# High and low halves of the weights in one tile, column by column

## The chip, the cores and the metric

The kernel runs on one NeuronCore of one Trainium2 chip. The metric is the device time of one execution in microseconds (us). TensorE (PE) multiplies; a matmul there is two instructions, a weight load (PEld in the profile), which puts up to 128 columns of the stationary operand into the array, and the matmul proper, which streams the moving operand past them. ScalarE (ACT) and VectorE (DVE) do the elementwise work, SyncE (SP) issues the transfers, and SBUF is the memory on the chip from which PE reads both operands: 128 partitions, and in each of them a row of bytes.

## The reference

One inference step of one decoder layer over 304 rows (16 meta tokens, 256 prompt rows, 8 sequences of 4 sampled rows) and a model width of 2048. Cut to what matters here:

```python
z = rms_norm(x, norm_mix) @ w_in                 # 2048 -> 3360 (RWKV-7) + 4096 (retention)
o = concat(rwkv7_mixer(z[..., :3360]), retention_mixer(z[..., 3360:]))
h = x + o @ w_out                                # 2048 -> 2048
hn = rms_norm(h, norm_ffn)
h = h + (silu(hn @ w_gate) * (hn @ w_up)) @ w_down   # 2048 -> 5632 -> 2048
y = rms_norm(h, norm_final)
```

Everything is float32. The two mixers (a recurrence over 64-wide heads, and chunked retention) need small matmuls and much elementwise work; the five big products with `w_in`, `w_out`, `w_gate`, `w_up` and `w_down` are nearly all of the arithmetic.

## The kernel before

**Splitting in halves.** Each weight and each activation is split into a high half, rounded to float32r, and a low half, the rest that the rounding left. A product is the sum of three matmuls into one PSUM bank: high weights by high activations, high by low, low by high (`main`, lines 723 to 725). The stationary operand is a block of 128 by 128 weights, the moving one 288 to 304 columns of activations, one column for each row of the input.

**The stream of weights.** All weights lie in `big` in the order of their use, cut into pieces of 128 x 512. `load` brings a piece into a ring `wr` of WR = 5 raw tiles. `cast` (line 666) makes the two halves: ACT copies the piece into a tile `wh` of type float32r (the high half), and `rest` lets DVE write `wl` = raw - high (the low half). `wh` and `wl` are two rings of WS = 5 tiles of 512 columns, 2 KB a partition each. One piece feeds four blocks of 128 columns, so twelve matmuls. In `main`, ACT's cast of a piece is issued three pieces ahead of the one in use, and DVE's subtraction half a piece later; only for the first nine pieces, while the input itself arrives, is each piece cast just before use.

**What sets the order.** `steps` lists the matmuls of the five products in one fixed order. Around them a planner (`Plan`) runs a draft of the whole program against estimated costs, notes which of the mixers' streams to advance when, and the real program repeats these decisions; on each engine the order of the program is kept. The draft knows of each operand only the box from its first to its last element.

**Where the tiles lie.** Scratch tiles share two arenas, one for float32, one for float32r. `Room.place` packs them, the float32r arena first (at most `WIDE` words) and the float32 arena into the `ROOM` words less that. The float32 arena lies first and is padded with `GAP` words, so that the float32r arena behind it starts at a chosen place. It holds the feed-forward activations `act`, whose used part starts `SHIFT_A` words into the tile: 0, 4, 8, ... 32, then 2 and 6 for the eleven groups of four blocks of `w_down`. For the products with `w_gate` and `w_up` the moving operands `xh` and `xl` have `SHIFT_X` = 4 * (k // 2) words, k being the block of rows. A word is 4 bytes.

Of the kernel before, what the change touches and what calls it, by code (L numbers as in the profile page):

```python
# [8 lines left out]
F32 = mybir.dt.float32  # L9
F32R = mybir.dt.float32r  # L10
# [5 lines left out]
P = 128  # L16
# [31 lines left out]
WS = 5  # L48
# [31 lines left out]
LASTK = T - P  # L80
KEYS = ((0, META, SEQ, 0), (P, P, NP - P, SEQ), (LASTK, 2 * P, T - 2 * P, SEQ + NP - P))
RMW = SEQ + NP - P + T - 2 * P
ROOM = 33040
GAP = 56
WIDE = 4200
FREE, GAPS, TRIES = 800.0, (2000.0, 1000.0, 500.0, 200.0, 50.0, 0.0), 12

# [215 lines left out]
class Timed:  # L303


    def __init__(self, plan, eng, name):
        self._plan, self._eng, self._name = plan, eng, name
# [280 lines left out]
class Step:  # L588


    def __init__(self, tc, I, O, ctx, rooms, draft, log):
        self.tc, self.nc, self.I, self.O = tc, tc.nc, I, O
        self.rooms, self.draft = rooms, draft
        pool = lambda n, b, **k: ctx.enter_context(tc.tile_pool(name=n, bufs=b, **k))
        self.cp = pool("const", 1)
        self.wp = pool("weights", 1)
        self.mp = pool("scratch", 1)
        self.ap_ = pool("acc", ACC, space=bass.MemoryType.PSUM)
        self.pp = pool("psum", 8 - ACC, space=bass.MemoryType.PSUM)
        self.n, self.tags = 0, {}  # L600
        self.plan = pl = Plan(self.nc, rooms, draft, log, (lambda i: i) if draft else tc.keep_in_program_order)
        self.sp = pl.sp
        if not draft:
            self.arena = {dt: self.mp.tile([P, r.size + (GAP if dt == F32 else 0)], dt, tag=f"arena_{dt}", name=f"arena_{dt}")
                          for dt, r in rooms.items()}
        self.pe, self.dve, self.act, self.pool = pl.pe, pl.dve, pl.act, pl.pool
        pl.outside = {v.name for v in (*I.values(), *O.values())}
        self.outs = []
        self.live = 0
        self.done = set()  # L610
# [53 lines left out]
        self.loaded += n  # L664

    def cast(self, parts=1):
        hi = self.t([P, 512], "wh", F32R, pool=self.wp, bufs=WS)
        lo = self.t([P, 512], "wl", F32R, pool=self.wp, bufs=WS)
        o = self.halved % WCOLS
        raw = self.raws[0][:, o:o + 512]  # L670
        n = 512 // parts
        part = [slice(c * n, (c + 1) * n) for c in range(parts)]
        for c in part:
            self.act.copy(hi[:, c], raw[:, c])
        self.halves.append((hi, lo))
        self.rests.append((lo, [(lo[:, c], raw[:, c], hi[:, c]) for c in part]))
        self.halved += 512
        if o + 512 == WCOLS:
            self.raws.pop(0)
# [1168 lines left out]
def body(tc, I, O):  # L1848
# [6 lines left out]
    rooms[F32R].place(WIDE)  # L1855
    rooms[F32].place(ROOM - rooms[F32R].size)
    with ExitStack() as ctx:
# [23 lines left out]
```

## Time and profile before

| | |
|---|---|
| time, median of 3 runs (lowest to highest) | 1549.97 us (1548.45 to 1550.41) |
| the profiled execution's own time | 1547.98 us |
| its span in the profile | 1546.2 us |
| granted PE clock over the span | 0.997 |
| PE / PEld busy | 99% / 97% |
| DVE / ACT / POOL busy | 70% / 56% / 2% |

The page of the profile lists the busy time of each engine, the span in 40 slices, the chain of work that ended last, and groups of instructions by name and shape. A matmul's recorded duration is longer than its share of the array's time, since the next one starts before it ends; so the time that a matmul costs is read here from the distance of one start to the next, as the timeline gives it, or as length of a window over the number of matmuls in it.

The kernel has two parts. Until about 600 us the products with `w_in` and `w_out` run among the small matmuls of the mixers, and DVE is busy for most of the time; from there to 1506 us PE does the feed-forward products almost alone.

### The profile page before, as it was taken

What the parts mean: (1) busy time and instruction counts of PE and PEld (TensorE: products, weight loads), DVE (VectorE), ACT (ScalarE), POOL (GpSimd) and SP (SyncE); (2) the same over time, 40 slices, a digit from 0 to 9 for tenths busy, and PEclk for the clock granted to TensorE, in tenths of its full rate; (3) what the DMA queues carried; (4) which work ended last, traced back from release to release, by engine and by line L of the source; (5) the groups of instructions that cost most, each with busy time, mean ns of one, the idle gap of its engine ahead of it and who ended that gap; (6) DMA issues with size and microseconds to landing.
All of it is one profiled execution on the core that took longest, in us unless ns stands there. A gap on an engine that the chain in (4) does not pass through costs nothing.

```text
span 1546.2 us, 31919 instructions
## 1 busy us (share of the span) xinstructions
PE 1530.1 (99%) x11446; PEld 1502.8 (97%) x11446; DVE 1089.9 (70%) x2782; ACT 866.5 (56%) x2031; POOL 27.7 (2%) x161
## 2 busy tenths in 40 slices
PE   9999999999999999999999999999999999999997
PEld 8999999999999989999999999999999999999997
DVE  6998789898899878676555565656565656565656
ACT  6775876787877765554444444444444444444446
POOL 1000000000000000000000000000000000000000
PEclk9999999999999999999999999999999999999998
DMA  7554445445434575655555555555655555655553
GB/s 243 163 148 140 131 110 155 120 115 170 155 117 150 170 262 190 207 165 164 169 165 169 165 167 171 163 170 159 171 165 169 165 166 166 173 159 172 161 171 116
DMA packets 136334, 252.33 MB, mean 163 GB/s; under 512 B 15984, under 2 KB 22256, under 8 KB 136176
## 3 DMA queue, kind: packets, MB, share of 16 engines
q1 hardware_dynamic: 136176, 250.29, 54.6%
q8 instruction: 91, 1.49, 0.4%
q14 instruction: 67, 0.55, 0.1%
HBM read 235.95 MB, written 14.28 MB: 162 GB/s over the span
## 4 chain that ended last, share of the span: by engine, by line
PE 93%; DVE 5%; ACT 1%; issue 1%; DMA 0%; SPq 0%; DVEq 0%; ACTq 0%
PE acc L314 82%; PE mm L314 11%; DVE arena_dt.float L314 3%; DVE wl L314 1%; DMA arena_dt.float<-xT 0%; SPq L314 0%; ACT arena_dt.float L314 0%; DVE arena_dt.float32r L314 0%; ACT arena_dt.float32r L314 0%; ACT wh L314 0%; DVE xl L314 0%; ACT xh L314 0%; DVEq L1877 0%; ACT shout L314 0%; DVEq L314 0%
## 5 line engine op out<-in xcount | busy, mean ns | idle before, releaser
L314 PE MATMUL acc<-xh,wh 128*128 128x288 f32 (+2 forms) x2592 | 790.6, 305 | 1.8 <-ACT wh L314 1.0
L314 PE MATMUL acc<-xl,wh 128*128 128x288 f32 (+2 forms) x2592 | 768.5, 296 | 0.1
L314 PE MATMUL acc<-xh,wl 128*128 128x288 f32 (+2 forms) x2592 | 766.4, 296 | 0.3 <-DVE wl L314 0.3
L314 ACT CAST wh<-wr 128x512 fp32r<-128x512 f32 (+1 forms) x827 | 501.4, 616 | 352.7 <-PE acc L314 313.2
L314 DVE TENSOR_TENSOR wl<-wr,wh 128x512 fp32r<-128x512 f32 (+1 forms) x827 | 560.3, 685 | 130.6 <-ACT wh L314 127.8
L314 PEld LDWEIGHTS acc<-xh,wh 128*128 128x128 f32 x2592 | 487.2, 188 | 8.7 <-issue 3.7
L314 PEld LDWEIGHTS acc<-xl,wh 128*128 128x128 f32 x2592 | 486.3, 188 | 4.5 <-issue 1.2
L314 PEld LDWEIGHTS acc<-xh,wl 128*128 128x128 f32 x2592 | 485.8, 187 | 0.9 <-DVE wl L314 0.6
L314 PE MATMUL acc<-arena_dt.float32r,wh 128*128 128x288 f32 x1408 | 280.6, 295 | 0.4 <-ACT arena_dt.float32r L314 0.3
L314 PEld LDWEIGHTS acc<-arena_dt.float32r,wh 128*128 128x128 f32 x1408 | 225.9, 188 | 0.8 <-ACT arena_dt.float32r L314 0.5
L314 PE MATMUL acc<-arena_dt.float32r,wl 128*128 128x288 f32 x704 | 207.7, 295 | 0.0
L314 DVE TENSOR_TENSOR arena_dt.float<-acc,arena_dt.float 128x288 f32<-128x288 f32 (+4 forms) x181 | 72.7, 419 | 168.5 <-PE acc L314 168.2
L314 DVE TENSOR_TENSOR arena_dt.float<-arena_dt.float 128x288 f32<-128x288 f32 (+22 forms) x694 | 175.1, 286 | 12.0 <-ACT arena_dt.float L314 7.6
L314 ACT ACTIVATE arena_dt.float<-arena_dt.float 128x288 f32<-128x288 f32 (+7 forms) x245 | 104.6, 433 | 117.0 <-DVE arena_dt.float L314 115.2
L314 PE MATMUL mm<-arena_dt.float 128*128 128x128 f32 (+7 forms) x1136 | 167.7, 302 | 0.6 <-issue 0.2
L314 DVE TENSOR_TENSOR arena_dt.float<-arena_dt.float,acc 128x288 f32<-128x288 f32 (+1 forms) x210 | 94.6, 451 | 97.3 <-PE acc L314 97.0
L314 PEld LDWEIGHTS mm<-arena_dt.float 128*128 128x128 f32 (+1 forms) x1136 | 141.3, 181 | 11.3 <-issue 3.6
L314 PEld LDWEIGHTS acc<-arena_dt.float32r,wl 128*128 128x128 f32 x704 | 132.4, 188 | 0.0
L314 ACT COPY arena_dt.float<-mm 64x64 f32<-64x64 f32 (+11 forms) x330 | 91.5, 286 | 49.1 <-PE mm L314 44.0
L314 ACT CAST arena_dt.float32r<-arena_dt.float 128x288 fp32r<-128x288 f32 (+4 forms) x73 | 30.5, 423 | 90.8 <-DVE arena_dt.float L314 90.3
L314 ACT COPY arena_dt.float<-arena_dt.float 128x32 f32<-128x32 f32 (+7 forms) x235 | 57.1, 293 | 13.3 <-DVE arena_dt.float L314 11.5
L314 DVE SCALAR_TENSOR_TENSOR arena_dt.float<-arena_dt.float 128x288 f32<-128x288 f32 (+3 forms) x96 | 43.1, 452 | 2.3 <-ACT arena_dt.float L314 0.5
(66 smaller groups left out, 563.0 us busy)
## 6 DMA issues: line engine op xcount, KB each, us to landing
wr<-big SPq DMA_DIRECT2D x823, 256.0 KB, 2.8
arena_dt.float<-s0r SPq DMA_DIRECT2D x16, 512.0 KB, 5.7
out_rts<-arena_dt.float SPq DMA_DIRECT2D x16, 512.0 KB, 4.6
arena_dt.float<-xT SPq DMA_DIRECT2D x4, 576.0 KB, 4.6
arena_dt.float<-lora SPq DMA_DIRECT2D x16, 128.0 KB, 2.6
arena_dt.float<-s0w SPq DMA_DIRECT2D x8, 256.0 KB, 3.0
out_rws<-arena_dt.float SPq DMA_DIRECT2D x8, 256.0 KB, 3.5
out_y<-arena_dt.float SPq DMA_DIRECT2D x7, 288.0 KB, 2.4
```

The source lines that it names most:

```text
L314: return self._plan.keep(f(*a, **k))
```

## The change

`wh` and `wl` become one tile `whl` of 1024 columns, of which the even ones are the high half and the odd ones the low half. What was a contiguous block of 128 columns (512 bytes) in every weight load, in ACT's write of the high half, and in DVE's read of it and write of the low half, is now every second word of 1024 bytes. The matmuls, their order, and what is written and read are the same. Beside it the padding of the float32 arena is worked out from its size, and the room for the arenas is 32 words less.

```diff
-ROOM = 33040
-GAP = 56
+ROOM = 33008
...
-            self.arena = {dt: self.mp.tile([P, r.size + (GAP if dt == F32 else 0)], dt, tag=f"arena_{dt}", name=f"arena_{dt}")
+            self.arena = {dt: self.mp.tile([P, r.size + ((16 - r.size) % 64 if dt == F32 else 0)], dt, tag=f"arena_{dt}", name=f"arena_{dt}")
...
     def cast(self, parts=1):
-        hi = self.t([P, 512], "wh", F32R, pool=self.wp, bufs=WS)
-        lo = self.t([P, 512], "wl", F32R, pool=self.wp, bufs=WS)
+        both = self.t([P, 1024], "whl", F32R, pool=self.wp, bufs=WS).rearrange("p (c q) -> p q c", q=2)
+        hi, lo = both[:, 0], both[:, 1]
```

## The prediction

> **What bounds the kernel now.** I read the page first: busy time by engine, granted clock, chain that ended last, costliest groups.
>
> ```profile
> PE 1530.1 (99%) x11446; PEld 1502.8 (97%) x11446; DVE 1089.9 (70%) x2782; ACT 866.5 (56%) x2031; POOL 27.7 (2%) x161
> ...
> PE 93%; DVE 5%; ACT 1%; issue 1%; DMA 0%; SPq 0%; DVEq 0%; ACTq 0%
> ...
> L314 PE MATMUL acc<-xh,wh 128*128 128x288 f32 (+2 forms) x2592 | 790.6, 305 | 1.8 <-ACT wh L314 1.0
> L314 PE MATMUL acc<-xl,wh 128*128 128x288 f32 (+2 forms) x2592 | 768.5, 296 | 0.1
> L314 PE MATMUL acc<-xh,wl 128*128 128x288 f32 (+2 forms) x2592 | 766.4, 296 | 0.3 <-DVE wl L314 0.3
> ```
>
> PE is the bound: 99% busy, 93% of the chain, and in these groups it stood idle for 2.2 us in all. So a change of the layout can win only where it shortens the distance from one matmul to the next. That distance comes from the windows (length; in brackets the number of instructions):
>
> ```profile
> core 0: us, PE busy (x) PEld busy (x) DVE busy (x) ACT busy (x) POOL busy (x), PEclk, DMA share, GB/s
> 0.00:600.00 600.00, 594.14 (x4375) 568.11 (x4376) 516.60 (x1732) 448.70 (x1278) 27.67 (x161) 1.00 0.51 157
> 600.00:1500.00 900.00, 900.00 (x6804) 899.51 (x6803) 542.66 (x988) 392.31 (x699) 0.00 (x0) 1.00 0.58 170
> 1500.00:1546.20 46.20, 35.96 (x272) 35.16 (x270) 30.63 (x63) 25.49 (x55) 0.00 (x0) 0.91 0.40 126
> ```
>
> From 600 to 1500 us there are 6804 matmuls in 900 us: 132.3 ns each, at a granted clock of 1.00, without a wait. The question is what these 132.3 ns are made of, and whether the layout of a weight load has a part in them. Two comparisons in the trace say that it has.
>
> The first: two stretches inside the products with w_down. The work is the same (288 columns, loads of 128 columns, same rings); what differs is where the moving operand starts against the weights: SHIFT_A is 12 words in the first, 20 in the second.
>
> ```profile
> 985.50:1010.10 24.60, 24.60 (x185) 1.00 0.52 157
> 1138.50:1163.10 24.60, 24.60 (x191) 1.00 0.60 158
> ```
>
> A record lasts 0.29 us, so about two in each count only reach into the window: 24.6 / 183 = 134.4 ns against 24.6 / 189 = 130.2 ns. A shift of 32 bytes is worth 4.2 ns a matmul. Stalls by address are thus part of the 132.3 ns.
>
> The second: the only matmuls with short loads, 32 columns instead of 128 (the third column block of the input projection, 290 columns moving).
>
> ```profile
> 12.33 0.29 PE L314 MATMUL acc<-xh,wh 128*32 128x290 f32 x1
> 12.46 0.29 PE L314 MATMUL acc<-xl,wh 128*32 128x290 f32 x1
> 12.59 0.29 PE L314 MATMUL acc<-xh,wl 128*32 128x290 f32 x1
> 12.72 0.29 PE L314 MATMUL acc<-xh,wh 128*32 128x290 f32 x1
> 12.85 0.29 PE L314 MATMUL acc<-xl,wh 128*32 128x290 f32 x1
> 12.98 0.29 PE L314 MATMUL acc<-xh,wl 128*32 128x290 f32 x1
> 13.11 0.30 PE L314 MATMUL acc<-xh,wh 128*32 128x290 f32 x1
> 13.25 0.29 PE L314 MATMUL acc<-xl,wh 128*32 128x290 f32 x1
> 13.38 0.30 PE L314 MATMUL acc<-xh,wl 128*32 128x290 f32 x1
> 13.51 0.30 PE L314 MATMUL mm<-xh,wh 128*128 128x304 f32 x1
> ```
>
> From 12.33 to 13.11 are six matmuls of 130 ns; the last three (13.11 to 13.51) take 133 ns. All nine stream 290 columns and load 32; the three slow ones load another 32 columns of the same tile. So the load's address counts too, by 3 ns, and only in one of the places. I read this as **meetings of load and stream**: both read SBUF at the same time, and where they come upon the same part of it the stream waits for some 3 ns. Without a meeting 290 columns take 130 ns, and 288 columns (2/290 less) 129.1 ns.
>
> How fast a load goes on is shown by its two sizes:
>
> ```profile
> L314 PEld LDWEIGHTS acc<-xh,wh 128*128 128x128 f32 x22 | 4.1, 188 | 0.0
> ...
> L314 PEld LDWEIGHTS acc<-xh,wh 128*32 128x32 f32 x16 | 1.7, 108 | 1.5 <-ACT wh L314 1.2
> ```
>
> 96 more columns take 80 ns: 0.83 ns a column, 107 ns for 128. The stream reads 288 columns in about 129 ns, 0.45 ns a column. A contiguous load therefore moves through memory at about half the stream's pace (4 bytes in 0.83 against 0.45 ns), and the stream overtakes it: a load of 128 columns is met about once wherever it starts.
>
> **The change part by part.**
>
> *Loads 8 bytes apart.* If a column still takes 0.83 ns, a load goes over 8 bytes in 0.83 ns, 9.6 bytes a ns, and the stream over 4 bytes in 0.45 ns, 8.9 bytes a ns: nearly the same pace. Then the stream hardly overtakes. It meets a load only where they start close to each other; the SHIFT values spread these starts, so most matmuls would see no meeting. I take the clean distance as between the two rows without much stall, 129.1 and 130.2 ns: 129.7 ns. The gain is 132.3 - 129.7 = 2.6 ns a matmul. No row shows a strided load, so the cost is bounded from both sides. Below: as long as the load keeps its pace, no layout goes under its own 107 ns, a gain of 25 ns; that end is far, the nearest rows are the short loads and the better stretch, and the value stays by them. Above: a load that takes twice as long (2 x 107 = 213 ns) would itself become the distance, 81 ns more.
>
> *How many matmuls.* From 600 to 1500 us all 6804 gain: 6804 x 2.6 = 17.7 us. Before that the large products have these shares (instructions that read a high half, and a low half):
>
> ```profile
> 0.00:600.00 600.00, 428.70 (x1953) 313.83 (x1954) 165.94 (x246) 148.46 (x248) 1.00 0.51 157
> ...
> 0.00:600.00 600.00, 291.28 (x976) 181.98 (x976) 165.94 (x246) 1.00 0.51 157
> ```
>
> 1953 + 976 = 2929, times 2.6 ns = 7.6 us. There DVE is at 516.6 of 600 us, and when PE gets faster the mixers' chains are late next, so I count half: 3.8 us. After 1500 us 272 x 2.6 = 0.7 us. Sum 22.2 us.
>
> *Writes 8 bytes apart.* ACT's cast and DVE's subtraction touch the same number of words. Rows of both (the subtraction, the cast, two of ACT's other copies):
>
> ```profile
> L314 DVE TENSOR_TENSOR wl<-wr,wh 128x512 fp32r<-128x512 f32 x823 | 558.7, 687 | 129.7 <-ACT wh L314 126.9
> L314 ACT CAST wh<-wr 128x512 fp32r<-128x512 f32 x823 | 499.9, 617 | 351.6 <-PE acc L314 313.2 <-ACT wh L314 28.2 <-DVE wl L314 2.3
> ...
> L314 ACT COPY arena_dt.float<-arena_dt.float 128x8 f32<-128x8 f32 x34 | 6.6, 199 | 0.5 <-PE mm L314 0.5
> ...
> L314 ACT CAST arena_dt.float32r<-arena_dt.float 128x256 fp32r<-128x256 f32 x16 | 6.4, 399 | 0.3 <-DMA arena_dt.float<-lora 0.3
> ```
>
> (617 - 399) / 256 = 0.85 ns a contiguous element, 181 ns fixed. Most of the copies of 8 elements write 20 bytes apart (the start values in `mixed`); they take 199 ns where the line gives 188. A stride costs between nothing and 11 / 8 = 1.4 ns an element, 0.7 us a cast. I take nothing, since most of 199 ns is the fixed part. What hides it from 600 us on:
>
> ```profile
> 1000.00 0.62 ACT L314 CAST wh<-wr 128x512 fp32r<-128x512 f32 x1 [0.98 <-PE acc L314]
> 1001.63 0.62 ACT L314 CAST wh<-wr 128x512 fp32r<-128x512 f32 x1 [1.00 <-PE acc L314]
> ```
>
> A cast is due every 1.6 us and ACT idles for 1 us of it. Before 600 us the cover is thin on DVE: 246 subtractions at 0.7 us more would be 172 us on top of 516.6 us, past the 600.
>
> *Waits.* The cast of a piece now waits until the low half's last matmul of five pieces before has run, not the high half's: one matmul, 0.13 us, hidden by the three pieces of lead. If the program's bookkeeping takes the interleaved halves for overlapping, the first matmul on a high half also waits for DVE's subtraction; with the lead it is done by then. Without lead, in the first nine pieces ((128 + 128 + 32) x 16 / 512), it costs at most a subtraction each, 9 x 0.687 us = 6 us; behind that matmul all of PE queues. PE would wait there for the low half two matmuls later anyway, so I take nothing. The float32r arena keeps its start modulo 64 words if the padding rule reproduces the 56; 32 words less room may move some scratch tiles: no instruction is added, so nothing.
>
> **The sum** is 1547.98 - 22.2 = 1525.8 us for the profiled execution. That execution lies 2.0 us under the median; so 1549.97 - 22.2 = 1527.8 us, rounded **1528 us**.
>
> **A rule to weigh.** The trace shows 130 against 133 ns in one tile, by the load's address. The Trainium skill ("TensorE: Matmul & The Clock Gate", Part 2, step 1) says that PE has two independent read ports and that loading the next weights does not steal SBUF bandwidth from the running matmul; by that rule the layout changes nothing and the time stays at 1550 us. The rows of the short loads speak against it here, but they are only nine matmuls. The Trainium skill ("SBUF — State Buffer", the box on cachelines under Door 1) has lines of 16 bytes, wants at least two hits in each for full bandwidth and puts a penalty on each change of line: 8 bytes apart gives fp32 two hits, so the load would keep its pace, but it changes line twice as often; no run here shows yet which half of the rule decides.
>
> **The rivals.**
>
> 1. *Each part of memory that a load touches costs, whatever the pace.* Then a load over 1024 bytes is met twice where one over 512 was met once. For it: the 32-column loads, which touch a quarter, are mostly free; short range and few meetings fit both readings. Against it: the pace of the two streams. Price: 2.6 ns more instead of less, all of it on PE: (6804 + 2929 + 272) x 2.6 = 26 us, **1576 us**, slower. It decides from the point at which the count of touched lines and not the relative pace sets the stalls. The same sign has a load that starts in step with the stream and stays so: a stall in every line rather than one.
> 2. *The load gets longer.* It has 132.3 - 107 = 25 ns of slack; a stride that makes it over 24% slower takes over the distance. At twice the time it is 81 ns x 10005 = 810 us, about 2360 us. Nothing in the trace speaks for it, nothing excludes it.
> 3. *The layout of loads does not matter*: stalls are the stream's own, and the differences above come from its address alone. 1550 us. Against it: the nine short loads.
> 4. *More than the meetings goes*: the better stretch still holds a meeting as large as the difference of the two, and the distance falls to 130.2 - 4.2 = 126 ns; 6 ns x (6804 + half of 2929 + 272) = 51 us, 1499 us. Neither window is that low.
> 5. *The strided writes are slow*: 516.6 + 172 - 600 = 89 us, 1639 us.
>
> **How the numbers follow.** Forecast (a gain of 1 to 4 ns a matmul) 0.47; rival 4 0.05; no effect 0.14; rival 1 0.23; rivals 2 and 5 0.11. A measurement here tells 0.2%, 3 us, from no change. Faster: 0.47 + 0.05, less a little for gains that drown: 0.51; same 0.15; slower 0.34. The forecast's own range is 1516 to 1541 (4 to 1 ns x 8.5 thousand effective matmuls, rounded). The range for 8 in 10 also takes in no change and rival 1: 1500 to 1580 us; the other 2 in 10 are mostly the long load and the slow writes.
>
> **What would show it.** In the window from 600 to 1500 us the distance should fall from 132.3 to about 129.7 ns; the two w_down stretches should change unequally. LDWEIGHTS should keep 188 ns; if it grows by 107 ns, rival 2 holds. The cast and the subtraction should stay at 617 and 687 ns, else rival 5. A distance of 135 ns at unchanged 188 ns is rival 1, of 132 ns rival 3. The prediction is wrong as a whole if PE no longer sets the pace after 600 us.

## The result, and the profile after

The changed kernel takes **1561.68 us** (median of 3, 1561.63 to 1563.53) against 1549.97 us: 1.0082 times, 95% interval 1.0059 to 1.0105. It is slower by 11.7 us, where 22 us less had been forecast. The time lies inside the range; the sign was wrong.

The windows of the changed kernel (length, busy time and in brackets the number of instructions by engine, granted clock, DMA):

```profile
0.00:600.00 600.00, 592.05 (x4319) 566.70 (x4320) 509.40 (x1716) 456.15 (x1272) 27.09 (x161) 1.00 0.50 154
600.00:1500.00 900.00, 900.00 (x6760) 898.70 (x6759) 544.32 (x992) 414.48 (x694) 0.00 (x0) 1.00 0.57 169
```

PE is still the bound, and after 600 us it is still busy without a break. There it does 6760 matmuls where it did 6804: 133.1 ns instead of 132.3, so 0.86 ns x 6804 = 5.9 us of the loss. (Up to about 700 us this window holds the rest of the product with `w_out`, and only from there on the feed-forward products.) In the first 600 us it does 56 fewer; at 600 us / 4375 = 137 ns each that is 7.7 us. The two make up the 13.5 us between the two spans (1559.7 and 1546.2 us).

The page's costliest groups say what became longer (busy us, mean ns of one, idle time before):

```profile
L313 PEld LDWEIGHTS acc<-xh,whl 128*128 128x128 f32 x5184 | 868.7, 195 | 9.1 <-issue 3.3
...
L313 ACT CAST whl<-wr 128x512 fp32r<-128x512 f32 (+1 forms) x827 | 539.4, 663 | 349.4 <-PE acc L313 303.2
L313 DVE TENSOR_TENSOR whl<-wr,whl 128x512 fp32r<-128x512 f32 (+1 forms) x827 | 562.0, 686 | 152.9 <-ACT whl L313 142.3
```

A weight load takes 195 ns instead of 188, a cast on ACT 663 instead of 616; DVE's subtraction is as long as before. And the two stretches of the products with w_down, with the moving operand 12 and 20 words into its row:

```profile
995.70:1020.30 24.60, 24.60 (x187) 1.00 0.54 157
1149.10:1173.70 24.60, 24.60 (x187) 1.00 0.52 155
```

Before they held 185 and 191 matmuls. Now both hold 187 (133 ns): the bad start got better, the good one got worse, and between these two the start of the stream no longer shows. That is not what "most matmuls would see no meeting" would look like. The start has not lost all its weight, though. These are the stretches with starts of 28 and of 2 words in the changed kernel:

```profile
1302.40:1327.00 24.60, 24.60 (x189) 1.00 0.58 160
1456.20:1480.80 24.60, 24.60 (x184) 1.00 0.54 152
```

In the kernel before the same two held 189 and 187 (24.60 us from 1290.90 and from 1443.30).

### The profile page after: what moved, and what is told of

Read it like the earlier page. It is cut to its first block, busy times and chain, and to the rows that moved or that the text cites. A ratio compares the mean times of both kernels' runs of the same rounds, so it can differ in the third digit from the quotient of the medians.

```text
span 1559.7 us, 31811 instructions
## 1 busy us (share of the span) xinstructions
PE 1542.0 (99%) x11446; PEld 1514.6 (97%) x11446; DVE 1091.4 (70%) x2782; ACT 902.6 (58%) x2031; POOL 27.1 (2%) x161
## 4 chain that ended last, share of the span: by engine, by line
PE 88%; DVE 7%; ACT 3%; issue 1%; DMA 1%; SPq 0%; DVEq 0%; ACTq 0%
PE acc L313 79%; PE mm L313 9%; DVE arena_dt.float L313 5%; ACT arena_dt.float L313 2%; DVE whl L313 1%; ACT whl L313 0%; SPq L313 0%; DMA arena_dt.float<-xT 0%; DMA wr<-big 0%; DMA arena_dt.float<-lora 0%; DVE arena_dt.float32r L313 0%; ACT arena_dt.float32r L313 0%; DVE xl L313 0%; ACT xh L313 0%; DVEq L1876 0%
## 5 line engine op out<-in xcount | busy, mean ns | idle before, releaser
L313 PE MATMUL acc<-xh,whl 128*128 128x288 f32 (+2 forms) x5184 | 1112.7, 302 | 1.9 <-ACT xh L313 0.8
L313 PEld LDWEIGHTS acc<-xh,whl 128*128 128x128 f32 x5184 | 868.7, 195 | 9.1 <-issue 3.3
L313 PE MATMUL acc<-xl,whl 128*128 128x288 f32 (+2 forms) x2592 | 771.4, 298 | 0.1
L313 ACT CAST whl<-wr 128x512 fp32r<-128x512 f32 (+1 forms) x827 | 539.4, 663 | 349.4 <-PE acc L313 303.2
L313 DVE TENSOR_TENSOR whl<-wr,whl 128x512 fp32r<-128x512 f32 (+1 forms) x827 | 562.0, 686 | 152.9 <-ACT whl L313 142.3
L313 PEld LDWEIGHTS acc<-xl,whl 128*128 128x128 f32 x2592 | 504.9, 195 | 4.1 <-issue 1.2
L313 PE MATMUL acc<-arena_dt.float32r,whl 128*128 128x288 f32 x2112 | 284.9, 297 | 0.4 <-ACT arena_dt.float32r L313 0.3
L313 PEld LDWEIGHTS acc<-arena_dt.float32r,whl 128*128 128x128 f32 x2112 | 283.3, 196 | 0.8 <-ACT arena_dt.float32r L313 0.5
L313 DVE TENSOR_TENSOR arena_dt.float32r<-arena_dt.float,arena_dt.float32r 128x288 fp32r<-128x288 f32 (+4 forms) x72 | 31.7, 440 | 1.8 <-ACT arena_dt.float32r L313 1.4
L313 DVE TENSOR_TENSOR arena_dt.float<-arena_dt.float,cst 128x256 f32<-128x256 f32 (+4 forms) x68 | 30.2, 473 | 3.9 <-ACT arena_dt.float L313 3.5
```

The source lines that it names most:

```text
L313: return self._plan.keep(f(*a, **k))
```

## The experiments

All ratios are against the kernel before, run on the same chip beside them. Unless it is said, the order of all instructions and the places of the scratch tiles are those of before.

### Loads alone, writes alone, both

*loads8*: the stored weights hold the columns of two blocks in turn, so `wh` and `wl` stay two tiles, casts stay contiguous, and only the load is strided.

```diff
+    big = big.reshape(P, -1, 2, P).transpose(0, 1, 3, 2)
...
+        return t[:, b * 256:(b + 1) * 256].rearrange("p (c q) -> p q c", q=2)[:, q, r:r + m]
...
-            self.pe.matmul(acc[:m, :n], hi[:, o:o + m], xh, start=k == 0, stop=False)
...
+            self.pe.matmul(acc[:m, :n], self.cols(hi, o, m), xh, start=k == 0, stop=False)
...
```

The other two matmuls of a block take their weights through `cols` in the same way.

> Kernel before with one thing changed: each pair of 128-column blocks lies interleaved in the stored weights, so that a load reads 128 columns 8 bytes apart; casts and subtractions stay contiguous, the order of all instructions is that of before. Theory A (the strided load costs on TensorE): about 1557 to 1562 us, loads of 195 ns instead of 188, distance from 600 to 1500 us 133.1 ns instead of 132.3, casts at 617 ns. Theory B (strided writes of the casts cost, and the changed plan): 1550 us, distance 132.3 ns.

*writes8*: the tile of the change, written as there, but each load takes 128 words in a row. It leaves out the sorting of the two halves: a load holds 64 high and 64 low columns, so the products are others, at the same amount of work.

```diff
+        t, at = t
+        b, r = divmod(o, P)
+        return t[:, b * 256 + at + r:b * 256 + at + r + m]
...
-            self.pe.matmul(acc[:m, :n], hi[:, o:o + m], xh, start=k == 0, stop=False)
...
+            self.pe.matmul(acc[:m, :n], self.cols(hi, o, m), xh, start=k == 0, stop=False)
...
```

> The interleaved tile of the change, written 8 bytes apart as in the change, order of instructions as before, but each load reads 128 contiguous words of it (so 64 high and 64 low columns: what the products compute is another thing, the work is the same). Theory A: 1550 us and 132.3 ns with loads of 188 ns, though casts take 663 ns. Theory B: 1554 to 1560 us, with the loss before 600 us.

*sameplan*: the change, but the draft sees the two old tiles.

```diff
+        if self.draft:
+            hi = self.t([P, 512], "wh", F32R, pool=self.wp, bufs=WS)
+            lo = self.t([P, 512], "wl", F32R, pool=self.wp, bufs=WS)
+        else:
+            both = self.t([P, 1024], "whl", F32R, pool=self.wp, bufs=WS)
...
```

> The change with the order of instructions and the places of all scratch tiles as before (the draft sees two separate tiles). If the changed order and the smaller room cost part of the 11.7 us, this one is faster than 1561.7 us by that part: by the share of the time lost before the products with w_out (5.4 us) at most, so 1556 to 1562 us. If order costs nothing, 1561.7 us.

It was run a second time beside the changed kernel itself:

> The changed kernel once more, beside the next one on the same chip: 1560 to 1562 us. What it has over the next kernel is the price of the changed order of instructions and places.

> The change with order and places of before: 1558 to 1559 us as in its first run. If its interval lies apart from that of the changed kernel, the order costs 2 to 3 us; if they overlap widely, nothing.

| kernel | median us | ratio, 95% interval | load / cast, ns |
|---|---|---|---|
| loads8 | 1557.36 | 1.0056 (1.0043 to 1.0069) | 195 / 616 |
| writes8 | 1550.21 | 1.0011 (1.0002 to 1.0020) | 188 / 660 |
| sameplan | 1558.48 | 1.0062 (1.0050 to 1.0075) | 195 / 663 |
| sameplan, again | 1558.34 | 1.0063 (1.0051 to 1.0076) | 195 / 663 |
| the change, again | 1561.92 | 1.0085 (1.0071 to 1.0099) | 195 / 663 |

The window from 600 to 1500 us, PE alone, of loads8, then of writes8:

```profile
600.00:1500.00 900.00, 900.00 (x6755) 1.00 0.56 168
```

```profile
600.00:1500.00 900.00, 900.00 (x6803) 1.00 0.56 169
```

Only strided loads cost PE anything there: 6755 against 6804 of before, as in the change; with strided writes and contiguous loads it is 6803. So **the strided loads cost 8.9 us** (1557.36 against 1548.43), three quarters of the loss, and **the strided writes 1.8 us** (1550.21 against 1548.43; the interval begins just above 1). The writes cost before 600 us, where writes8 does 4363 matmuls against 4375, and it is ACT's casts that got longer, 660 ns against 616. Their sum, 10.7 us, is about what sameplan loses, 10.1 us. What the change has over sameplan in the same series, 1561.92 - 1558.34 = **3.6 us**, comes with the order of instructions and the places that the draft chose anew: it sees the boxes of the two halves overlap, and there are 32 words less of room. The section on the change says that the order of the matmuls stays; it does not. Read in order by name and shape, 391 of the 11446 places in PE's order hold another matmul than before, and in sameplan none. The intervals of the two overlap a little (from 1.0071 to 1.0076); their runs do not (1561.76 to 1562.64 and 1558.01 to 1560.27). The window from 400 to 600 us, PE alone, of the change and of sameplan, both again, shows where:

```profile
400.00:600.00 200.00, 196.28 (x1431) 1.00 0.50 169
```

```profile
400.00:600.00 200.00, 197.89 (x1449) 1.00 0.51 172
```

Which of order and places it is was not tried.

### Is it the start of the stream?

*sh20* and *sh12* give every moving operand of the feed-forward products one and the same start, with contiguous loads; *loads8_sh20* does it with loads 8 bytes apart.

```diff
-SHIFT_X = [4 * (k // 2) for k in range(KT)]
-SHIFT_A = [0, 4, 8, 12, 16, 20, 24, 28, 32, 2, 6]
+SHIFT_X = [20] * KT
+SHIFT_A = [20] * 11
```

> Kernel before (contiguous loads) with every moving operand of the feed-forward products 20 words into its row, the place of the better one of the two stretches. If a distance is set by where stream and load start against each other, all of the feed-forward products take that stretch's 130.0 to 130.2 ns instead of 132.3: 2.2 ns x 6800 = 15 us less, 1535 us. If the 130.2 ns were peculiar to that stretch, 1550 us.

> The same starts with loads 8 bytes apart. Theory L (load and stream at one pace lock, and an equal start gives one distance wherever it is): exactly 133.3 ns from 600 to 1500 us, as in most w_down stretches of the changed kernel, so 1557 to 1561 us. If the start matters for this pace too, something else than 133.3 ns.

> Contiguous loads, every moving operand of the feed-forward products 12 words into its row, the place of the worse of the two stretches. If the start alone sets the distance: about 134.5 ns from 600 to 1500 us, 15 us more than before, 1564 us. If the change from one start to the next matters as much: 131 to 133.3 ns.

Window of sh20, of sh12, and of loads8_sh20:

```profile
600.00:1500.00 900.00, 900.00 (x6860) 1.00 0.56 171
```

```profile
600.00:1500.00 900.00, 900.00 (x6697) 1.00 0.54 167
```

```profile
600.00:1500.00 900.00, 900.00 (x6748) 1.00 0.55 168
```

sh20 takes 1540.7 us, 0.9948 (0.9933 to 0.9963), at 900 us / 6860 = 131.2 ns; sh12 1564.68 us, 1.0103 (1.0083 to 1.0123), at 134.4 ns. With contiguous loads the start moves the distance. The first 100 us of these windows still hold the product with `w_out`, whose starts are as before, so here are the feed-forward products alone, of the kernel before, of sh20 and of sh12:

```profile
800.00:1500.00 700.00, 700.00 (x5293) 1.00 0.58 167
```

```profile
800.00:1500.00 700.00, 700.00 (x5342) 1.00 0.55 168
```

```profile
800.00:1500.00 700.00, 700.00 (x5200) 1.00 0.53 163
```

These are 132.3, 131.1 and 134.7 ns. sh12 takes what its stretch had shown. sh20 does not come down to the 130.2 ns of its stretch, not even in that stretch itself, which now holds 189 matmuls where it held 191:

```profile
1135.40:1160.00 24.60, 24.60 (x189) 1.00 0.51 157
```

So the start alone does not set the distance; it looks as if what surrounds a stretch counts too, but no run singles that out. With loads 8 bytes apart the same start gives 133.4 ns and 1557.84 us, 1.0057 (1.0040 to 1.0073), as theory L had it: the good start is gone.

*alt64* and *loads8_alt64* let the starts of consecutive moving operands differ by 64 bytes in turn; *after_alt64* does it in the changed kernel.

```diff
+                s = 16 * (f % 2)
...
+                hi, lo = hl[:, 0, s:s + TO], hl[:, 1, 16 - s:16 - s + TO]
...
-        self.xf = [(xh[:, k, s:s + TO], xl[:, k, s:s + TO]) for k, s in enumerate(SHIFT_X)]
+        self.xf = [(xh[:, k, s:s + TO], xl[:, k, 16 - s:16 - s + TO]) for k, s in enumerate([0, 16] * 8)]
```

> Kernel before with the starts of consecutive moving operands 64 bytes apart in turn (high half at 0, low half at 64, and the other way round for the next block), contiguous loads. If distances come in units of a turn of 128 bytes (13.3 ns at 9.6 bytes a ns), starts 64 bytes apart allow half units: 126.7 ns, 5.6 ns x 6800 = 38 us less, 1512 us, or 140 ns, 1602 us. If only the mean matters, near 1550 us.

> The same starts with loads 8 bytes apart. Theory L: the lock holds in half units, exactly 126.7 ns (1514 us) or exactly 140.0 ns (1604 us). Against L: about 133 ns, 1557 us, as with the starts of before.

> The changed kernel with the starts of consecutive moving operands 64 bytes apart. If the price of the strided loads is a matter of the starts, 10 us less than the changed kernel, 1551 us, at 131.7 ns from 600 to 1500 us and casts still at 663 ns; if the two do not add up, 1560 us.

Window of alt64, of loads8_alt64, and of after_alt64:

```profile
600.00:1500.00 900.00, 900.00 (x6807) 1.00 0.55 170
```

```profile
600.00:1500.00 900.00, 900.00 (x6824) 1.00 0.56 170
```

```profile
600.00:1500.00 900.00, 900.00 (x6753) 1.00 0.55 168
```

The idea of whole and half turns of 128 bytes, and theory L with it, fell: neither 126.7 nor 140 ns came, but 132.2 (alt64, 1547.54 us, 0.9992, 0.9983 to 1.0002) and 131.9 ns (loads8_alt64, 1547.32 us, 0.9993, 0.9983 to 1.0002). Yet loads8_alt64 is 10.0 us faster than loads8, with loads just as strided (194 ns). So **the price of loads 8 bytes apart is not paid for each load**; it hangs on how starts and loads follow each other. It can even turn into a gain. Here are the first 600 us and the feed-forward products, of alt64 and then of loads8_alt64:

```profile
0.00:600.00 600.00, 594.46 (x4375) 1.00 0.50 157
720.00:1500.00 780.00, 780.00 (x5901) 1.00 0.55 167
```

```profile
0.00:600.00 600.00, 594.50 (x4359) 1.00 0.50 156
720.00:1500.00 780.00, 780.00 (x5927) 1.00 0.55 167
```

With these starts the strided loads do 26 matmuls more among the feed-forward products than the contiguous ones, and 16 fewer in the first 600 us, where the starts are those of before; the equal times hide a gain and a loss. Nor is there a simple remedy: in the changed kernel the same starts give 133.3 ns and 1562.11 us, 1.0090 (1.0076 to 1.0103), and the two prices, of the loads and of the starts, do not add up. On PE the two kernels differ, besides the order before 600 us, in which loads begin 4 bytes further. In the changed kernel it is each low half; in loads8_alt64 it is the second block of each pair, in both halves.

*low8* strides the low halves alone; DVE writes them 8 bytes apart.

```diff
+            by = lambda a: a.rearrange("p (b q c) -> p b q c", q=2, c=P)
+            two = lambda a: a.rearrange("p (b c q) -> p b q c", q=2, c=P)
-        self.rests.append((lo, [(lo[:, c], raw[:, c], hi[:, c]) for c in part]))
+            self.rests.append((lo, [(two(lo[:, c]), by(raw[:, c]), by(hi[:, c])) for c in part]))
...
-            self.pe.matmul(acc[:m, :n], lo[:, o:o + m], xh, start=False, stop=k == K - 1)
+            self.pe.matmul(acc[:m, :n], self.cols(lo, o, m), xh, start=False, stop=k == K - 1)
```

> Only the low halves are interleaved by pairs of blocks (DVE writes them 8 bytes apart), so one load in three is strided; starts as before. If each strided load costs on its own (7 ns of load, 0.9 ns of distance), a third of the loss: 132.6 ns, 1551.5 us. If the loss comes from stream and load at one pace in every matmul, less than a third or nothing: 1548.5 to 1550 us. DVE's subtraction at 687 ns if strided writes are free for it.

It takes 1553.97 us, 1.0034 (1.0021 to 1.0047), which is 5.3 us, more than a third of the loss of loads8 (3.0 us, and the interval begins at 3.3): neither expectation holds. Its loads and subtractions, min/median/max ns:

```profile
L314 PEld LDWEIGHTS acc<-xh,wl x2592: 106/195/200, 5.5 to 1511.9; 128*128 128x128 f32 x199, 128*32 128x32 f32 x1
...
L314 DVE TENSOR_TENSOR wl<-wr,wh x827: 418/686/708, 4.0 to 1533.2; 128x512 fp32r<-128x512 f32 x165, 128x256 fp32r<-128x256 f32 x1
```

The median strided load is 7 ns longer here too (195 against 188), and the strided write costs DVE nothing.

### How far can a load be spread?

*loads16* interleaves four blocks; *loads12* three of the four blocks of a piece, the fourth stays contiguous. The loads pick their columns accordingly.

```diff
+    big = big.reshape(P, -1, 4, P).transpose(0, 1, 3, 2)
```

```diff
+    four = big.reshape(P, -1, 4, P)
+    three = four[:, :, :3].transpose(0, 1, 3, 2).reshape(P, -1, 3 * P)
+    big = np.concatenate([three, four[:, :, 3]], 2).reshape(P, -1)
```

> As the first, but four blocks interleaved: a load reads 128 columns 16 bytes apart. If a load is paced by columns only, it looks like the 8-byte one: loads of about 195 ns, 1557 to 1562 us. If it is paced by lines of 16 bytes (the Trainium skill, SBUF page, box on cachelines, wants two hits in each), a load of 128 lines takes longer, up to twice the 107 ns of its columns: loads of up to 300 ns, distance up to 213 ns, 2300 us. In the first piece the products wait for the second half of the cast, under 1 us.

> Three of the four blocks of a piece interleaved, so three loads in four read 128 columns 12 bytes apart; order and casts as before. Theory S (a load takes at most one 16-byte line each 1.67 ns, as the 16-byte loads at about 213 ns say; at 8 bytes 64 lines need 107 ns, just the 107 ns of the columns, so there is no slack left and each meeting with the stream delays the load): 96 lines need 160 ns, a strided distance of 165 to 178 ns, 1800 to 1900 us. Theory P (the price at 8 bytes comes from load and stream at the same pace in bytes): at 12 bytes the load runs ahead of the stream, the pace differs again, 1545 to 1560 us.

> The 16-byte loads once more, for a profile in the state in which four of five executions took 2533 us: by theory S loads last 81 + 128 x 1.67 = 294 ns and matmuls follow at 213 to 235 ns. The one profiled execution so far took 8098 us, with loads of 851 ns.

loads12 takes 1855.63 us, 1.1984 (1.1961 to 1.2008); loads16 2532.82 us, 1.6349 (1.6327 to 1.6371). Weight loads of loads12 in order of time (start us, length us), within a run of strided ones:

```profile
1000.94 0.27 PEld L317 LDWEIGHTS acc<-xl,wh 128*128 128x128 f32 x1
...
1002.17 0.27 PEld L317 LDWEIGHTS acc<-xh,wl 128*128 128x128 f32 x1
```

and of the second look at loads16:

```profile
999.88 0.33 PEld L315 LDWEIGHTS acc<-xl,wh 128*128 128x128 f32 x1
...
1001.98 0.33 PEld L315 LDWEIGHTS acc<-xl,wh 128*128 128x128 f32 x1
```

Seven loads in 1.23 us are 175.7 ns each, nine in 2.10 us 233.3 ns. In lines of 16 bytes these loads touch 96 and 128: 1.83 and 1.82 ns a line. These three strides fit one rule: a load is paced by its columns (0.83 ns) or by its lines (1.82 ns, with matmuls streaming), whichever takes longer. Theory S of loads12's expectation holds, and the pace against the stream is not what decides at 12 bytes. At 8 bytes the rule gives 64 lines x 1.82 = 117 ns, an estimate, against the columns' 107: the lines would be just the slower of the two. Measured, the load grows by 7 ns (114 ns, by 195 less the fixed 188 - 107 = 81).

## Why the prediction was wrong

**What held.** PE bounds the kernel before and after. The distance of matmuls depends on the addresses of load and stream (sh20 and sh12 lie 24 us apart and differ in the starts alone; loads8 and the kernel before differ in the loads alone). The short loads show it as well: the trace has four batches of twelve, not nine matmuls alone, and in each batch the last three take 133 ns. The waits, taken at nothing, stayed small: PE waits 0.3 us for DVE's low halves in both kernels. The count of matmuls that turns a distance into a time was right (0.86 ns there, 5.9 us).

**The step that failed** is the first of the change part by part: that a load which keeps the stream's pace is hardly met, so that most matmuls run at the clean distance of 129.7 ns. The rows behind the 129.7 ns were nine matmuls with short loads and one stretch with a good start, all with contiguous loads; that strided loads would get there was concluded from the pace alone. The reading had a crack before that: if a contiguous load is met about once wherever it starts, a start cannot move the distance from 134.4 to 130.2 ns, as the two stretches show.

In its place the runs show that loads 8 bytes apart bring most starts to one distance near 133.3 ns: 187 matmuls in both stretches, and 133.4 ns in loads8_sh20 (the starts of 28 and 2 words are exceptions). With contiguous loads the starts gave values on both sides of that, 130.2 and 134.4 ns in the two stretches, with a mean of 132.3. The change lost the good ones with the bad ones, and the mean rose by 0.86 ns instead of falling by 2.6. Why it settles there, and why starts 64 bytes apart move it to 131.9 ns in one arrangement of the halves and not in the other, stays open.

**The assumption that the load keeps its pace** held nearly: the load is 7 ns longer, which the lines explain if the rule from loads12 and loads16 holds at 8 bytes too. It left 133 - 114 = 19 ns of slack, so the long load did not become the bound (rival 2); with four bytes more of stride, in loads12, it did.

**Rival 1** named the right sign and place, but not the mechanism or the size: 26 us were priced for two meetings a load; the strided loads cost 8.9 us. If each part of memory that a load touches had its own price, loads8_alt64 would not be as fast as the kernel before, and its feed-forward products would not be faster than those of alt64.

**Rival 3**, that the layout of the loads does not matter, is refuted in this kernel: loads8 differs from the kernel before in the loads alone and loses 0.56%, though its loads are well short of the distance. The prediction had drawn the same forecast from the rule of the Trainium skill ("TensorE: Matmul & The Clock Gate", Part 2, step 1) that a load does not take bandwidth from the running matmul. The runs do not agree with that forecast; whether it is bandwidth that the load takes, no run here shows. The other rule, two hits in each 16-byte line for full bandwidth (the Trainium skill, "SBUF — State Buffer", the box on cachelines under Door 1), nearly agrees with the runs: with two words in each line a load loses 7 ns of 188, and with four words on three lines or one on each it runs at about 1.82 ns a line.

**Strided writes**, taken at nothing, cost ACT 663 - 616 = 47 ns a cast, 0.09 ns an element (bound: 1.4), and the kernel 1.8 us; DVE nothing. The term was sized right for DVE and too low for ACT in the part before 600 us. The prediction had seen the thin cover there on DVE, and it was ACT's casts that cost.

**Order and places**, also taken at nothing since no instruction is added, cost 3.6 us. "No instruction is added" is no reason: a draft that sees other dependences lays the same instructions in another order.

Together that is 8.9 + 1.8 + 3.6 = 14.3 us, beside 11.7 us and 13.2 us in the two measurements of the change; the parts add up to no better than 1 to 3 us.

**Better than both kernels** is sh20, whose only edit is one start for all moving operands: 1540.7 us, 0.52% under the kernel before.

## What to carry to other kernels

Where PE is the bound and every matmul brings its own load, the distance of matmuls should be measured in stretches that differ only in the operands' addresses: here 32 bytes were worth 24 us, more than the layout change, and setting one measured start did better than spreading starts. In this kernel a load that used half of each 16-byte line was at the edge, and one that used less set the pace. A few matmuls that look clean show that a stall exists, not that another layout avoids it.

## What was unexpected of the hardware

Five of six executions of the kernel with loads 16 bytes apart took 2533 us; one, a profiled one, took 8098 us. In it the matmuls of the large products were slow alike, at a granted clock of 1.00. Its window (PE, PEld, DVE, ACT, POOL, clock, DMA):

```profile
600.00:1500.00 900.00, 900.00 (x1180) 872.20 (x1180) 141.59 (x532) 119.27 (x341) 6.81 (x39) 1.00 0.08 23
```

900 us / 1180 = 763 ns a matmul, and the loads of `wh` for the products with `xh` last 851 ns in the mean, where the other profiled execution has 327. But PE was slow before the first load 16 bytes apart, which starts at 13.8 us there. These are the first twenty matmuls, on a tile of ones with contiguous loads (start us, length us), of the long execution and of the other one:

```profile
1.05 13.76 PE L315 MATMUL mm<-ones 128*128 128x128 f32 x20 [1.05 <-DVE ones L315]
```

```profile
1.05 4.64 PE L315 MATMUL mm<-ones 128*128 128x128 f32 x20 [1.05 <-DVE ones L315]
```

DVE's subtractions (686 ns) and ACT's casts (615 ns) were as fast as ever. So it was PE that was slow, from its first matmul on, while the profile names a full clock, and the strided loads did not set it off. What did was not tried. In the kernels with loads 8 bytes apart nothing of the kind was seen.
